# A fp32r decoder trunk: priority for the chain between two projections in the order of VectorE and ScalarE

## The chip, the cores and the metric

The kernel runs on one core of a Trainium2 chip. Its time is the device time of one execution in microseconds. The core has a matmul engine (TensorE, PE in the profile; its weight loads are PEld), a vector engine (VectorE, DVE), a scalar engine (ScalarE, ACT), GpSimd (POOL) and a queue engine (SyncE, SP) that issues DMAs. Each engine works through its own list of instructions in order and waits on semaphores for the others.

## The reference

One inference step of a two-layer trunk of width 1024 over 512 prompt tokens and 8 x 4 sample tokens, in float32. Layer 0 mixes tokens with a gated linear recurrence (RG-LRU, width 1536), layer 1 with a chunked spatial gate. Each is followed by an MLP of width 4096 with a squared ReLU. What matters here stands between two matmuls:

```python
        x = x + g_m * rmsnorm(mix, norm_g[layer, 1])
        hf = rmsnorm(x, norm_g[layer, 2]) * (1.0 + sc_f) + sh_f
        f = jnp.square(jax.nn.relu(hf @ mlp_w_up[layer])) @ mlp_w_down[layer]
        x = x + g_f * rmsnorm(f, norm_g[layer, 3])
```

The output of one projection is normalised over the width, scaled and added to x; x is normalised again, scaled and shifted; only then can the next projection begin. This is called the chain below. It occurs between two projections three times: recurrent block to MLP of layer 0 (site A, about 324 to 357 us), MLP of layer 0 to the spatial gate's input projection (site B, about 752 to 785 us), spatial gate to MLP of layer 1 (site C, about 1010 to 1043 us).

## The kernel before

**Matmuls.** Activations lie with the width on 128 partitions, eight tiles k of 128 x 544 tokens (`X`, `MIX`, `HH`, `HL`). The tokens are two halves of 272 columns, h=0 (prompt) and h=1 (the rest of the prompt, 240 columns, and 32 sample columns). Every product is done in three passes: with `hi` and `lo` the rounded weight and its remainder, and `HH` and `HL` the same of the activation, it adds `hi`·`HH`, `lo`·`HH` and `hi`·`HL` (L119, one 128x128 weight tile by 272 columns). Two outputs of 272 columns share an accumulator tile `acc` of two PSUM banks; there are three such tiles.

**Weights.** SyncE's DMAs bring them in pieces of 512 KB (`raw`). `Unit.pieces` splits each in halves of 512 columns: ScalarE's cast writes `hi` (L181), VectorE's subtraction writes `lo` (L182); 404 of each. `Stream` writes them some 70 matmuls (`LS`) ahead of their use.

**The chain.** `final_proj` adds the last parts of a projection into `MIX` (L746, VectorE), two tiles k at a time; `Stat` squares them (L366, ScalarE), adds the squares up (L378 to L385, VectorE, `sq` and `pt`) and TensorE averages over the partitions (L391, `aux`). `rstd` makes 1/rms in `R` (L413, L414 on ScalarE, L415, L416 on VectorE). `Chain.run` does this for one half h: after `rstd` the residual, per k (L661 and L663 on VectorE; for h=1 the sample columns first, L654 to L656), squares and a second statistic, then per k the `scale` (L449, VectorE), `HH` (L453, ScalarE) and `HL` (L454, VectorE); the sample columns pass through `HSM` (L435 to L445). `first_sweeps` reads `HH` and `HL` k by k, first all of h=0, then all of h=1. The MLP's accumulators are evacuated by ScalarE (`hf`, L1265). At the start of the kernel the same scales and casts make the input of the first projection's x part (`hin_full`), beside `gt`, the evacuation of the gate part (L947), and `MOD`, the shift, which comes from the ada matmuls (L581, L591, L569).

**What sets the order.** The program is written with a clock that counts matmuls; tasks on it write the chain and the splits between the matmuls. The framework's scheduler then simulates the engines and takes, for each engine, among the instructions that are ready the one written first. `high_priority(offset=n)` makes what is written inside count as written n instructions earlier.

Of the kernel before, what the change touches and what calls it, by code (L numbers as in the profile page):

```python
# [80 lines left out]
def trunk_kernel(  # L81
# [266 lines left out]
    class Stat:  # L348
# [7 lines left out]
        def add(self, src, delay=6):  # L356
            i = self.n % 2
            if i == 0:
                self.cur = slot("sq")[:, 0:T].rearrange("p (j n) -> p j n", j=2)
            A.activation(self.cur[:, i], src, AF.Square)  # L360
            self.n += 1
            if i:
                self.q.append((clk.now + delay, self.cur))

        def add2(self, src, q, delay=6):
            A.activation(q, src, AF.Square)  # L366
            self.n += 2
            self.q.append((clk.now + delay, q))

        def pump(self):  # L370
            for i in range(KD // 2):
                while not clk.forced and (len(self.q) <= i or self.q[i][0] > clk.now):
                    yield 2
                q = self.q[i][1]
                if i == 0:
                    acc_ = q
                elif i == 1:
                    V.tensor_tensor(acc_, acc_, q, op=ALU.add)  # L378
                elif i == 2:
# [30 lines left out]
    def rstd(out, ms):  # L410

        t_ = slot("rs")[:, 0:HW]
        A.activation(out, ms, AF.Abs_reciprocal_sqrt, bias=epsc)  # L413
        A.activation(t_, out, AF.Square)  # L414
        V.scalar_tensor_tensor(t_, ms, EPS, t_, op0=ALU.add, op1=ALU.mult)  # L415
        V.scalar_tensor_tensor(out, t_, -3.0, out, op0=ALU.add, op1=ALU.mult)  # L416
# [7 lines left out]
    def smp(ap):  # L424
        return ap.rearrange("p k (s t) -> p k s t", t=TS)

    def smp_mod(m):
        n = m.shape[1]
        return m[:, :, 1:9].rearrange("p k (s o) -> p k s o", o=1).to_broadcast([P, n, NS, TS])
# [26 lines left out]


# [172 lines left out]
    class Chain:  # L630
# [976 lines left out]
```

## Time and profile before

| | us |
|---|---|
| median of 3 runs | 1432.56 (1431.56 to 1432.67) |
| the profiled execution | 1433.34 |
| its span | 1431.6 |
| TensorE busy in the span | 1393.1 (97%) |
| VectorE busy | 702.8 (49%) |
| ScalarE busy | 630.5 (44%) |

The profile is one execution with times from the span's start; the execution takes 1.7 us more than the span. Matmuls are pipelined: one of 272 columns is listed with 0.29 us, and the next one starts 0.125 us after it. The time in square brackets behind a row is what its engine was idle before it, and the arrow names the instruction that ended the wait. The granted clock is TensorE's, 1.00 for 2.4 GHz and 0.50 for 1.2 GHz.

### The profile page before, as it was taken

The numbers are of one execution on the slowest core, as the hardware profiler recorded it, in microseconds if no ns is written. First come the engines' busy times: TensorE is split into PE (matmuls) and PEld (weight loads), VectorE is DVE, ScalarE is ACT, GpSimd is POOL, SyncE is SP. The second block draws the span as 40 slices with busy tenths as digits, with TensorE's granted clock in tenths as the row PEclk, the third lists the DMA queues.
The fourth block names the chain that finished last, engine by engine and source line by source line (L and its number), as shares of the span: only waits on it lengthen the run. The fifth ranks groups of instructions, "written<-read, shape, count | busy, mean of one in ns | idle before, by whom it ended". The sixth has DMA issues, their size and how long they took to land.

```text
span 1431.6 us, 26339 instructions
## 1 busy us (share of the span) xinstructions
PE 1393.1 (97%) x11130; PEld 1298.9 (91%) x11130; DVE 702.8 (49%) x1442; ACT 630.5 (44%) x1154; POOL 41.5 (3%) x76
## 2 busy tenths in 40 slices
PE   8999999997999999999998999999899999999997
PEld 6899989997999999999997867999899999999996
DVE  4767476779422332333349346654972233333334
ACT  4465746846523413414425434432573341432523
POOL 1200000000100000000000200000000000000000
PEclk8999999999999999999999999999999999999998
DMA  9554544221545545543222333122232223222201
GB/s 308 177 175 127 163 151 149 103 89 60 181 154 173 172 155 174 171 155 117 61 87 60 91 96 111 65 71 69 83 101 90 89 89 89 90 89 89 89 1 63
DMA packets 129152, 165.66 MB, mean 116 GB/s; under 512 B 10168, under 2 KB 105416, under 8 KB 129034
## 3 DMA queue, kind: packets, MB, share of 16 engines
q1 hardware_dynamic: 127274, 161.89, 36.0%
q0 software_dynamic: 1760, 2.09, 0.7%
q8 instruction: 87, 1.43, 0.4%
q14 instruction: 31, 0.25, 0.1%
HBM read 161.31 MB, written 2.65 MB: 115 GB/s over the span
## 4 chain that ended last, share of the span: by engine, by line
PE 64%; issue 26%; DVE 6%; ACT 2%; DMA 1%; POOL 0%; SPq 0%; POOLq 0%; ACTq 0%; DVEq 0%
PE acc L119 58%; PE aux L610 3%; DVE lo L182 1%; PE acc L1494 1%; DVE MIX L449 1%; DVE HL L454 1%; DVE X L663 1%; DMA xsr<-in_x_sample_dram 1%; PE aux L1396 0%; PE aux L581 0%; DVE MIX L661 0%; PE aux L391 0%; DVE rs L415 0%; DVE R L416 0%; PE aux L1362 0%
## 5 line engine op out<-in xcount | busy, mean ns | idle before, releaser
L119 PE MATMUL acc<-HH,hi 128*128 128x272 f32 x1776 | 397.5, 292 | 12.3 <-ACT HH L453 11.2
L182 DVE TENSOR_TENSOR lo<-raw,hi 128x512 fp32r<-128x512 f32 (+1 forms) x404 | 263.9, 683 | 269.1 <-ACT hi L181 205.5
L119 PE MATMUL acc<-HH,lo 128*128 128x272 f32 x1776 | 391.7, 291 | 3.4 <-DVE lo L182 3.4
L181 ACT CAST hi<-raw 128x512 fp32r<-128x512 f32 (+1 forms) x404 | 230.2, 613 | 299.8 <-PE acc L119 174.4
L119 PE MATMUL acc<-HL,hi 128*128 128x272 f32 x1776 | 355.4, 289 | 3.3 <-DVE HL L454 3.3
L119 PEld LDWEIGHTS acc<-HH,hi 128*128 128x128 f32 x1776 | 292.2, 190 | 23.7 <-ACT HH L453 14.2
L119 PEld LDWEIGHTS acc<-HH,lo 128*128 128x128 f32 x1776 | 291.2, 190 | 11.6 <-issue 6.7
L119 PEld LDWEIGHTS acc<-HL,hi 128*128 128x128 f32 x1776 | 273.6, 188 | 10.7 <-issue 5.4
L119 PE MATMUL acc<-hh,lo 128*128 128x272 f32 x1024 | 229.8, 290 | 0.0
L119 PE MATMUL acc<-hh,hi 128*128 128x272 f32 x1024 | 229.7, 290 | 0.0
L119 PE MATMUL acc<-hl,hi 128*128 128x272 f32 x1024 | 229.4, 289 | 0.0
L119 PEld LDWEIGHTS acc<-hh,lo 128*128 128x128 f32 x1024 | 168.1, 188 | 3.7 <-issue 3.6
L119 PEld LDWEIGHTS acc<-hh,hi 128*128 128x128 f32 x1024 | 167.9, 188 | 3.9 <-issue 3.8
L119 PEld LDWEIGHTS acc<-hl,hi 128*128 128x128 f32 x1024 | 168.1, 188 | 3.6 <-issue 3.6
L1268 DVE TENSOR_TENSOR hl<-hf,hh 128x544 fp32r<-128x544 f32 (+1 forms) x76 | 47.7, 634 | 175.2 <-ACT hh L1267 175.1
L1265 ACT ACTIVATE hf<-acc 128x544 f32<-128x544 f32 (+1 forms) x76 | 41.2, 551 | 128.0 <-PE acc L119 126.1
L711 DVE TENSOR_TENSOR MIX<-MIX,acc 128x544 f32<-128x544 f32 x44 | 31.5, 717 | 76.0 <-PE acc L119 75.9
L119 PE MATMUL acc<-yh,hi 128*128 128x272 f32 x208 | 52.6, 290 | 0.3 <-ACT MIX L709 0.3
L119 PE MATMUL acc<-yh,lo 128*128 128x272 f32 x208 | 52.5, 291 | 0.0
L119 PE MATMUL acc<-yl,hi 128*128 128x272 f32 x208 | 52.3, 289 | 0.0
L709 ACT COPY MIX<-acc 128x544 f32<-128x544 f32 x32 | 19.6, 612 | 64.1 <-PE acc L119 64.1
L366 ACT ACTIVATE sq<-MIX 128x544 f32<-128x544 f32 x27 | 17.5, 656 | 65.8 <-DVE MIX L746 65.8
(332 smaller groups left out, 1410.8 us busy)
## 6 DMA issues: line engine op xcount, KB each, us to landing
ada<-in_ada_w_dram SPq DMA_DIRECT2D x96, 512.0 KB, 4.8
raw<-in_mlp_w_up_dram SPq DMA_DIRECT2D x64, 512.0 KB, 4.2
raw<-in_mlp_w_down_dram SPq DMA_DIRECT2D x64, 512.0 KB, 4.7
raw<-in_lru_w_in_dram SPq DMA_DIRECT2D x24, 512.0 KB, 4.3
raw<-in_sg_w_in_dram SPq DMA_DIRECT2D x24, 512.0 KB, 4.1
raw<-in_sg_w_out_dram SPq DMA_DIRECT2D x12, 512.0 KB, 4.3
raw<-in_lru_w_out_dram SPq DMA_DIRECT2D x8, 384.0 KB, 3.3
raw<-in_lru_w_out_dram SPq DMA_DIRECT2D x6, 512.0 KB, 5.7
```

The lines of the kernel that those rows point to most:

```text
L119: nc.tensor.matmul(out, lhsT, rhs, start=start, stop=stop)
L181: A.copy(h_, raw[:, c:c + st])
L182: V.tensor_tensor(l_, raw[:, c:c + st], f32(h_), op=ALU.subtract)
L366: A.activation(q, src, AF.Square)
L449: V.scalar_tensor_tensor(wv, X[:, k, c0:c1], Am[:, k, 0:1], R[:, c0:c1], op0=ALU.mult, op1=ALU.mult)
L454: V.scalar_tensor_tensor(HL[:, k, c0:c1], wv, sh[:, k, 0:1], f32(HH[:, k, c0:c1]), op0=ALU.add, op1=ALU.subtract)
L610: nc.tensor.matmul(ps[32 * g:32 * g + 32, :], scT[:, k, :], ts_[g // 2][:, (g % 2) * 512:(g % 2) * 512 + 512], start=(k == 0), stop=(k == ...
L663: V.scalar_tensor_tensor(X[:, j, c0:c1], MIX[:, j, c0:c1], Gm[:, j, 0:1], X[:, j, c0:c1], op0=ALU.mult, op1=ALU.add)
L709: A.copy(mv, ps[:, :, 0:HW])
L711: V.tensor_tensor(mv, mv, ps[:, :, 0:HW], op=ALU.add)
L1265: A.activation(dw, ps, AF.Relu)
L1268: V.tensor_tensor(dl, dw, f32(dh), op=ALU.subtract)
```

## The change

A wrapper gives every instruction that is issued through it a priority offset of 600. `Vp` and `Ap` are VectorE and ScalarE behind this wrapper, and the chain's instructions are issued through them: the squares and adds of `Stat`, `rstd`, the sample columns (`smp_split`, `smp_scale`, `smp_shift`), `scale`, `shift_split`, the residual in `Chain.run`, and the adds and copies from the accumulators in `mix_add` and `final_proj`. The weight splits, the MLP's and the gates' evacuations and all matmuls and DMAs are issued as before.

```diff
+PRIO = 600
+class First:
+    def __init__(self, tc, eng):
+        self.tc, self.eng = tc, eng
+    def __getattr__(self, name):
+        f = getattr(self.eng, name)
+        def call(*args, **kw):
+            with self.tc.high_priority(offset=PRIO):
+                return f(*args, **kw)
+        return call
...
+    Vp, Ap = First(tc, V), First(tc, A)
...
     def shift_split(sh, k, c0, c1):
         wv = MIX[:, k, c0:c1]
-        A.activation(HH[:, k, c0:c1], wv, AF.Identity, bias=sh[:, k, 0:1])
-        V.scalar_tensor_tensor(HL[:, k, c0:c1], wv, sh[:, k, 0:1], f32(HH[:, k, c0:c1]),
+        Ap.activation(HH[:, k, c0:c1], wv, AF.Identity, bias=sh[:, k, 0:1])
+        Vp.scalar_tensor_tensor(HL[:, k, c0:c1], wv, sh[:, k, 0:1], f32(HH[:, k, c0:c1]),
                                op0=ALU.add, op1=ALU.subtract)
...
-                        V.tensor_tensor(mv, mv, ps[i // 2][:, :, 0:HW], op=ALU.add)
+                        Vp.tensor_tensor(mv, mv, ps[i // 2][:, :, 0:HW], op=ALU.add)
```

On each engine the instructions are the same ones; 215 rows of VectorE, 173 of ScalarE and 802 of TensorE stand elsewhere, those of GpSimd and SyncE do not. In the new program a prioritised instruction is listed under the wrapper's line, L60, and other lines are 20 higher (L182 is L202, L119 is L139, L391 is L411).

VectorE at site A, before, around the weight split `lo_473` (the weights of k 4 to 7 for the second pair of output tiles); `sq` and `pt` are the first statistic of h=1, `L415` its rstd three rows after the last one shown:

```order
L382 TENSOR_TENSOR pt_468_3952<-sq_453_3813 128x272
L182 TENSOR_TENSOR lo_470_3964<-raw_449_3769,hi_469_3963 128x512
L454 SCALAR_TENSOR_TENSOR HL_91<-MIX_93,MOD0_95,HH_90 128x272
L746 TENSOR_TENSOR MIX_93<-MIX_93,acc_467_3937 128x2x272
L182 TENSOR_TENSOR lo_473_3995<-raw_450_3771,hi_472_3994 128x512 x2
L384 TENSOR_TENSOR pt_468_3952<-pt_468_3952,sq_471_3992 128x272
L449 SCALAR_TENSOR_TENSOR MIX_93<-X_89,MOD0_95,R_94 128x272
L385 TENSOR_TENSOR pt_468_3952<-pt_468_3952,sq_471_3992 128x272
L449 SCALAR_TENSOR_TENSOR MIX_93<-X_89,MOD0_95,R_94 128x272
L454 SCALAR_TENSOR_TENSOR HL_91<-MIX_93,MOD0_95,HH_90 128x272
L182 TENSOR_TENSOR lo_479_4044<-raw_458_3861,hi_478_4043 128x512
```

The same place now:

```order
L60 SCALAR_TENSOR_TENSOR rs_477_4027<-aux_476_4024,rs_477_4027 128x272
L60 SCALAR_TENSOR_TENSOR HL_91<-MIX_93,MOD0_95,HH_90 128x272
L60 SCALAR_TENSOR_TENSOR R_94<-rs_477_4027,R_94 128x272
L202 TENSOR_TENSOR lo_473_3995<-raw_450_3771,hi_472_3994 128x512
L60 TENSOR_TENSOR us_480_4050<-MIX_93,R_94 128x256
L60 TENSOR_TENSOR MIX_93<-MIX_93,R_94 128x2x240
...
L60 TENSOR_TENSOR MIX_93<-MIX_93 128x2x272
L60 SCALAR_TENSOR_TENSOR X_89<-MIX_93,MOD0_95,X_89 128x240 x2
L60 TENSOR_TENSOR HSM_92<-X_89,MOD0_95 128x256
L60 TENSOR_TENSOR pt_481_4103<-MIX_93 128x272
L202 TENSOR_TENSOR lo_473_3995<-raw_450_3771,hi_472_3994 128x512
L60 TENSOR_TENSOR pt_481_4103<-pt_481_4103,MIX_93 128x272
```

Before, both halves of `lo_473` stand in the middle of h=0's scales. Now the first half stands just before `us` (the start of h=1's residual), and the second behind that residual, the sums of its squares and the first of their folds.

TensorE at site A, before, from the matmul of h=1's first statistic; `acc_474` and `acc_475` are the first two accumulators of the MLP:

```order
L391 MATMUL aux_476_4024<-pt_468_3952,dmean_80 128x272
L119 MATMUL acc_474_4000<-HH_90,hi_464_3925 128x272
L119 MATMUL acc_474_4000<-HH_90,lo_465_3926 128x272
...
L119 MATMUL acc_475_4001<-HH_90,hi_472_3994 128x272
L119 MATMUL acc_475_4001<-HH_90,lo_473_3995 128x272
...
L119 MATMUL acc_474_4000<-HL_91,hi_462_3889 128x272 x4
L119 MATMUL acc_474_4000<-HL_91,hi_464_3925 128x272 x2
L119 MATMUL acc_475_4001<-HL_91,hi_469_3963 128x272 x4
L119 MATMUL acc_475_4001<-HL_91,hi_472_3994 128x272 x2
```

The same place now:

```order
L411 MATMUL aux_476_4024<-pt_468_3952,dmean_80 128x272
...
L139 MATMUL acc_474_4000<-HL_91,hi_462_3889 128x272 x2
L139 MATMUL acc_475_4001<-HH_90,lo_473_3995 128x272
...
L139 MATMUL acc_474_4000<-HL_91,hi_462_3889 128x272 x2
L139 MATMUL acc_474_4000<-HL_91,hi_464_3925 128x272 x4
L139 MATMUL acc_474_4000<-HL_91,hi_462_3889 128x272 x4
L139 MATMUL acc_474_4000<-HL_91,hi_464_3925 128x272 x4
L139 MATMUL acc_498_4203<-HH_90,hi_478_4043 128x272
L139 MATMUL acc_475_4001<-HH_90,lo_473_3995 128x272
```

Before, the matmuls with `lo_473` follow soon after the statistic and all come ahead of the HL matmuls. Now those of its first half come later, then 14 HL matmuls and one with `acc_498` (the third pair of outputs), and then the first one with its second half, the last row.

VectorE at the start of the kernel, before, from the second `R` on:

```order
L416 SCALAR_TENSOR_TENSOR R_94<-rs_74_539,R_94 128x272
L947 TENSOR_TENSOR gt_75_544<-acc_41_277,R_94 128x544
L182 TENSOR_TENSOR lo_77_547<-raw_48_288,hi_76_546 128x512
L867 TENSOR_TENSOR HSM_92<-HSM_92,R_94 128x128
L182 TENSOR_TENSOR lo_79_551<-raw_48_288,hi_78_550 128x512
L449 SCALAR_TENSOR_TENSOR MIX_93<-X_89,MOD0_95,R_94 128x512
L182 TENSOR_TENSOR lo_81_555<-raw_49_290,hi_80_554 128x512
L449 SCALAR_TENSOR_TENSOR MIX_93<-X_89,MOD0_95,R_94 128x512
L182 TENSOR_TENSOR lo_83_559<-raw_49_290,hi_82_558 128x512
L947 TENSOR_TENSOR gt_85_619<-acc_42_278,R_94 128x544
L569 TENSOR_TENSOR MOD0_95<-aux_87_623,G1_164 128x36
L449 SCALAR_TENSOR_TENSOR MIX_93<-X_89,MOD0_95,R_94 128x512
```

The same place now (a sample row and a split left out):

```order
L60 SCALAR_TENSOR_TENSOR R_94<-rs_74_539,R_94 128x272
L60 SCALAR_TENSOR_TENSOR MIX_93<-X_89,MOD0_95,R_94 128x512 x8
L967 TENSOR_TENSOR gt_75_544<-acc_41_277,R_94 128x544
L202 TENSOR_TENSOR lo_77_547<-raw_48_288,hi_76_546 128x512
L887 TENSOR_TENSOR HSM_92<-HSM_92,R_94 128x128
L202 TENSOR_TENSOR lo_79_551<-raw_48_288,hi_78_550 128x512
L202 TENSOR_TENSOR lo_81_555<-raw_49_290,hi_80_554 128x512
L967 TENSOR_TENSOR gt_85_619<-acc_42_278,R_94 128x544
L589 TENSOR_TENSOR MOD0_95<-aux_87_623,G1_164 128x36
L967 TENSOR_TENSOR gt_88_666<-acc_43_279,R_94 128x544
L60 TENSOR_TENSOR HSM_92<-HSM_92,MOD0_95 128x128
L60 SCALAR_TENSOR_TENSOR HL_91<-MIX_93,MOD0_95,HH_90 128x512 x4
```

All eight scales of the x projection's input have moved ahead of `gt`, the splits and the `MOD` that the casts need; before, two stood ahead of `MOD`.

## Rows read from the trace of the kernel before

**Rows 1.** The page, part 1: busy us (share of span), instructions, by engine.
```profile
PE 1393.1 (97%) x11130; PEld 1298.9 (91%) x11130; DVE 702.8 (49%) x1442; ACT 630.5 (44%) x1154; POOL 41.5 (3%) x76
```

**Rows 2.** TensorE's waits: total us, times, longest, by what ended them.
```profile
PE acc L119 <- ACT HH L453: 11.2, 8, 3.0
PE aux L391 <- DVE pt L385: 3.8, 3, 1.8
PE acc L119 <- DVE lo L182: 3.4, 4, 1.0
PE acc L119 <- DVE HL L454: 3.3, 3, 1.1
```

**Rows 3.** Timeline of TensorE, site A: start, duration, [idle before and its releaser].
```profile
323.88 0.29 PE L119 MATMUL acc<-HH,lo 128*128 128x272 f32 x1
...
327.19 0.39 PE L119 MATMUL acc<-HH,hi 128*128 128x272 f32 x1 [3.03 <-ACT HH L453]
...
348.26 0.39 PE L391 MATMUL aux<-pt,dmean 128*128 128x272 f32 x1
...
353.17 0.39 PE L119 MATMUL acc<-HH,hi 128*128 128x272 f32 x1 [0.92 <-ACT HH L453]
...
355.15 0.39 PE L119 MATMUL acc<-HH,hi 128*128 128x272 f32 x1 [0.71 <-ACT HH L453]
```

**Rows 4.** Timeline of VectorE, site A.
```profile
324.11 0.44 DVE L415 SCALAR_TENSOR_TENSOR rs<-aux,rs 128x272 f32<-128x272 f32 x1
324.46 0.72 DVE L378 TENSOR_TENSOR sq<-sq,sq 128x544 f32<-128x544 f32 x1
...
326.08 1.33 DVE L449 SCALAR_TENSOR_TENSOR MIX<-X,MOD,R 128x272 f32<-128x272 f32 x3
...
330.97 1.30 DVE L182 TENSOR_TENSOR lo<-raw,hi 128x512 fp32r<-128x512 f32 x2
...
337.26 0.43 DVE L654 TENSOR_TENSOR us<-MIX,R 128x256 f32<-128x256 f32 x1
...
345.67 0.45 DVE L382 TENSOR_TENSOR pt<-MIX 128x272 f32<-128x272 f32 x1
...
349.90 0.44 DVE L415 SCALAR_TENSOR_TENSOR rs<-aux,rs 128x272 f32<-128x272 f32 x1 [1.54 <-ACT rs L414]
```

**Rows 5.** Timeline of ScalarE, site A: the second evacuation of an MLP accumulator.
```profile
350.98 0.39 ACT L1265 ACTIVATE hf<-acc 128x272 f32<-128x272 f32 x1
```

**Rows 6.** Timelines of VectorE and TensorE, site B.
```profile
766.39 0.41 DVE L654 TENSOR_TENSOR us<-MIX,R 128x256 f32<-128x256 f32 x1
...
781.17 0.62 PE L1396 MATMUL aux<-raw,HSM 128*32 128x512 f32 x1 [0.67 <-DVE HSM L445]
```

**Rows 7.** Timeline of TensorE, site C.
```profile
1013.74 0.39 PE L119 MATMUL acc<-HH,hi 128*128 128x272 f32 x1 [3.02 <-ACT HH L453]
...
1039.73 0.39 PE L119 MATMUL acc<-HH,hi 128*128 128x272 f32 x1 [1.79 <-ACT HH L453]
```

**Rows 8.** Stretches at A and C: us, busy us by engine (x), granted clock, DMA.
```profile
327.19:331.30 4.11, 4.11 (x32) 4.11 (x33) 4.11 (x10) 2.02 (x5) 0.00 (x0) 1.00 0.06 12
1014.86:1018.27 3.41, 3.41 (x18) 3.41 (x17) 3.41 (x8) 1.66 (x4) 0.00 (x0) 0.50 0.11 14
```

**Rows 9.** Timelines of VectorE and TensorE, the start.
```profile
45.32 0.72 DVE L947 TENSOR_TENSOR gt<-acc,R 128x544 f32<-128x544 f32 x1
...
50.53 0.18 DVE L569 TENSOR_TENSOR MOD<-aux,G 128x36 f32<-128x36 f32 x1
...
55.91 2.73 DVE L449 SCALAR_TENSOR_TENSOR MIX<-X,MOD,R 128x512 f32<-128x512 f32 x4
...
53.80 0.42 PE L119 MATMUL acc<-HH,lo 128*128 128x272 f32 x2
...
59.01 1.51 PE L581 MATMUL aux<-ada,scT 128*32 128x128 f32 x46
...
61.41 0.52 PE L119 MATMUL acc<-HH,hi 128*128 128x272 f32 x2 [0.19 <-ACT hi L181]
```

More of the change, by code (lines that the diff above doesn't have):

```diff
@@ L359, in add @@
                 self.cur = slot("sq")[:, 0:T].rearrange("p (j n) -> p j n", j=2)
-            A.activation(self.cur[:, i], src, AF.Square)
+            Ap.activation(self.cur[:, i], src, AF.Square)
             self.n += 1
@@ L365, in add2 @@
         def add2(self, src, q, delay=6):
-            A.activation(q, src, AF.Square)
+            Ap.activation(q, src, AF.Square)
             self.n += 2
@@ L377, in pump @@
                 elif i == 1:
-                    V.tensor_tensor(acc_, acc_, q, op=ALU.add)
+                    Vp.tensor_tensor(acc_, acc_, q, op=ALU.add)
                 elif i == 2:
-                    V.tensor_tensor(acc_, acc_, q, op=ALU.add)
+                    Vp.tensor_tensor(acc_, acc_, q, op=ALU.add)
                     p = slot("pt")
-                    V.tensor_tensor(p[:, 0:HW], acc_[:, 0], acc_[:, 1], op=ALU.add)
+                    Vp.tensor_tensor(p[:, 0:HW], acc_[:, 0], acc_[:, 1], op=ALU.add)
                 else:
-                    V.tensor_tensor(p[:, 0:HW], p[:, 0:HW], q[:, 0], op=ALU.add)
-                    V.tensor_tensor(p[:, 0:HW], p[:, 0:HW], q[:, 1], op=ALU.add)
+                    Vp.tensor_tensor(p[:, 0:HW], p[:, 0:HW], q[:, 0], op=ALU.add)
+                    Vp.tensor_tensor(p[:, 0:HW], p[:, 0:HW], q[:, 1], op=ALU.add)
             if self.rows:
@@ L412, in rstd @@
         t_ = slot("rs")[:, 0:HW]
[L413 to L416, printed above, removed]
+        Ap.activation(out, ms, AF.Abs_reciprocal_sqrt, bias=epsc)
+        Ap.activation(t_, out, AF.Square)
+        Vp.scalar_tensor_tensor(t_, ms, EPS, t_, op0=ALU.add, op1=ALU.mult)
+        Vp.scalar_tensor_tensor(out, t_, -3.0, out, op0=ALU.add, op1=ALU.mult)
     def newton_rstd(out, v, tmp):
@@ L434, in smp_split @@
     def smp_split(k0, k1):
-        A.copy(HH[:, k0:k1, SEQ:T], HSM[:, k0:k1])
-        V.tensor_tensor(HL[:, k0:k1, SEQ:T], HSM[:, k0:k1], f32(HH[:, k0:k1, SEQ:T]), op=ALU.subtract)
+        Ap.copy(HH[:, k0:k1, SEQ:T], HSM[:, k0:k1])
+        Vp.tensor_tensor(HL[:, k0:k1, SEQ:T], HSM[:, k0:k1], f32(HH[:, k0:k1, SEQ:T]), op=ALU.subtract)
     def smp_scale(Am, k0, k1):
@@ L440, in smp_scale @@
         w3 = HSM[:, k0:k1]
-        V.tensor_tensor(smp(w3), smp(X[:, k0:k1, SEQ:T]), smp_mod(Am[:, k0:k1]), op=ALU.mult)
-        V.tensor_tensor(w3, w3, R[:, None, SEQ:T].to_broadcast([P, n, NSMP]), op=ALU.mult)
+        Vp.tensor_tensor(smp(w3), smp(X[:, k0:k1, SEQ:T]), smp_mod(Am[:, k0:k1]), op=ALU.mult)
+        Vp.tensor_tensor(w3, w3, R[:, None, SEQ:T].to_broadcast([P, n, NSMP]), op=ALU.mult)
     def smp_shift(sh, k0, k1):
-        V.tensor_tensor(smp(HSM[:, k0:k1]), smp(HSM[:, k0:k1]), smp_mod(sh[:, k0:k1]), op=ALU.add)
+        Vp.tensor_tensor(smp(HSM[:, k0:k1]), smp(HSM[:, k0:k1]), smp_mod(sh[:, k0:k1]), op=ALU.add)
     def scale(Am, k, c0, c1):
         wv = MIX[:, k, c0:c1]
-        V.scalar_tensor_tensor(wv, X[:, k, c0:c1], Am[:, k, 0:1], R[:, c0:c1], op0=ALU.mult, op1=ALU.mult)
+        Vp.scalar_tensor_tensor(wv, X[:, k, c0:c1], Am[:, k, 0:1], R[:, c0:c1], op0=ALU.mult, op1=ALU.mult)
     def shift_split(sh, k, c0, c1):
         wv = MIX[:, k, c0:c1]
-        A.activation(HH[:, k, c0:c1], wv, AF.Identity, bias=sh[:, k, 0:1])
-        V.scalar_tensor_tensor(HL[:, k, c0:c1], wv, sh[:, k, 0:1], f32(HH[:, k, c0:c1]),
+        Ap.activation(HH[:, k, c0:c1], wv, AF.Identity, bias=sh[:, k, 0:1])
+        Vp.scalar_tensor_tensor(HL[:, k, c0:c1], wv, sh[:, k, 0:1], f32(HH[:, k, c0:c1]),
                                op0=ALU.add, op1=ALU.subtract)
@@ L653, in run @@
                 w3 = w[:, 0:KD * NSMP].rearrange("p (k s) -> p k s", k=KD)
-                V.tensor_tensor(w3, MIX[:, :, SEQ:T], R[:, None, SEQ:T].to_broadcast([P, KD, NSMP]), op=ALU.mult)
-                V.tensor_tensor(smp(w3), smp(w3), smp_mod(Gm), op=ALU.mult)
-                V.tensor_tensor(X[:, :, SEQ:T], X[:, :, SEQ:T], w3, op=ALU.add)
+                Vp.tensor_tensor(w3, MIX[:, :, SEQ:T], R[:, None, SEQ:T].to_broadcast([P, KD, NSMP]), op=ALU.mult)
+                Vp.tensor_tensor(smp(w3), smp(w3), smp_mod(Gm), op=ALU.mult)
+                Vp.tensor_tensor(X[:, :, SEQ:T], X[:, :, SEQ:T], w3, op=ALU.add)
                 yield 8
@@ L713, in final_proj @@
     def final_proj(lhs, rhs, both, groups, l, idx, nxt):
-        A.activation(warm, epsc, AF.Abs_reciprocal_sqrt)
+        Ap.activation(warm, epsc, AF.Abs_reciprocal_sqrt)
         S = [Stat(), Stat(nxt is None)]
@@ L735, in final_proj @@
                         mm3(ps, lhs(m), rhs, (1,), col=0)
-                        V.tensor_tensor(MIX[:, m, HS[1]], MIX[:, m, HS[1]], ps[:, 0, 0:HW], op=ALU.add)
+                        Vp.tensor_tensor(MIX[:, m, HS[1]], MIX[:, m, HS[1]], ps[:, 0, 0:HW], op=ALU.add)
                         S[1].add(MIX[:, m, HS[1]])
```

4 lines of the change are left out of this document (2 added, 2 removed).

## The prediction

> **What bounds the kernel now.** I read the page first. TensorE is busy 97% of the span, VectorE 49%, ScalarE 44% [rows 1]: only TensorE's waits can be won, and whatever makes it wait longer is lost. The view of waits comes next. The waits that end on the chain's instructions are those on ScalarE's HH casts (L453), on the statistic's last add (L385) and on VectorE's HL (L454); a fourth ends on the weight split `lo` (L182) [rows 2]. The timeline of TensorE shows where they stand. At the first seam (recurrent block to MLP, "site A") it waits 3.03 us before the first HH matmul and twice in the h=1 sweep (0.92 and 0.71) [rows 3], and between these once for HL and once for `lo` (1.1 and 1.0 are the longest of [rows 2]). The aux wait of [rows 2] and such waits at site B (MLP to spatial gating) [rows 6] and site C (spatial gating to MLP) [rows 7] bring the groups of [rows 2] to 11.2 + 3.8 + 3.4 + 3.3 = 21.7 us. That is all that the change could win. VectorE's timeline says why they are there: between 324.11 and about 348 it is never idle [rows 4]. On a full engine priority cannot shorten the row of work, only choose who is late.
>
> **What moves.** Every engine issues the same instructions as before, so no duration is added or removed. The front part's rows show what changes place. At site A in the new order VectorE does the whole chain of h=0, then the whole residual of h=1, and the second half of one weight split, `lo_473`, comes only near the end of that residual. TensorE reaches the matmul that reads it much sooner, and it works in order: nothing behind it can run.
>
> **Site A, step by step.** All prices are VectorE's durations in [rows 4] less the 0.09 us by which the next instruction starts early (L415 took 0.44, L378 starts 0.35 later): 0.63 us for a 544-wide add, 0.61 for `lo`, 0.41 for a 272-wide scale or HL, 0.35 for a short add or rstd step.
> (1) The add of the last pair (L746) now stands ahead of L415 of h=0. Its accumulator ends with the matmul at 323.88 + 0.29 = 324.17 [rows 3], so L415 starts at about 324.17 + 0.63 = 324.8, against 324.11: the first HH matmul comes 0.7 us later, 327.9 for 327.19.
> (2) From L415 of h=0 to L654 (the start of h=1's residual) the new order has 2 `lo`, 8 scales, 8 HL and the statistic: 2 x 0.61 + 16 x 0.41 + 2 x 0.63 + 7 x 0.35 = 11.5 us. L654 starts at 336.3 instead of 337.26: a gain of 0.9.
> (3) From L654 to the statistic's folding add (L382) before took 345.67 - 337.26 = 8.4 us, with two HL (0.82) that have now moved ahead and without one 0.34 us sample scale that has moved in: 7.9, and 0.35 for L382 itself. The second `lo_473` starts at about 336.3 + 8.3 = 344.6 and ends at 345.3. Before, that pair of `lo` ran from 330.97 to 332.27 [rows 4].
> (4) TensorE. The first half of `lo_473` stands just ahead of L654, done at 336.4; behind it are 8 matmuls, 14 of HL and one HH, at the pitch of 0.125 us: 336.4 + 23 x 0.125 = 339.3. There it waits until 345.3, **6.0 us idle**, where before no wait on `lo` was longer than 1.0 [rows 2].
> (5) What is left of h=0 then: 8 + 16 + 31 + 16 = 71 matmuls (8.9 us), an aux (0.3) and seven transposes at the same pitch (0.9): 355.4. The h=1 sweep also needs an accumulator, and its evacuation, L1265 at 350.98 before [rows 5], now stands behind all eight HH casts of h=1. The statistic matmul of h=1 comes at 346.7 for 348.26 [rows 3], its rstd at 348.4 for 349.90 [rows 4]; then VectorE needs 0.8 us for R and the sample's product and some 0.37 us (240 wide: between the 0.35 and 0.41 above) for each of 8 scales, 8 HL and four more sample steps, 7.4 us for the 20: 356.6 at the last HL, with the eighth HH just before it on ScalarE and the evacuation right behind. So h=1 starts at about **356.7**, and then without a wait. Before it started at 353.17 and lost 0.87 more inside (0.71 at 355.15 and the slower first matmul after a wait, 0.39 for 0.29) [rows 3], effectively 354.04. Site A: 356.7 - 354.0 = **+2.7 us**. The waits for HL and those of 0.92 and 0.71 us do go; the long one takes their place.
>
> **Sites C and B.** C is A moved by 686.55 us (1013.74 against 327.19). Before, its h=1 sweep started at 1039.73, with the same 0.87 lost inside [rows 7]: 1040.6, against 356.7 + 686.5 = 1043.2 now: **+2.6 us**. At B the second half of `lo_921` has moved behind the residual too. L654 stood at 766.39 there [rows 6]; with the 0.9 us gain, the 8.3 of step 3 and the 0.7 of the `lo` itself it ends near 774.5, and 71 matmuls and an aux (9.2) end h=0 at 783.7, against 781.17 when the sample's matmul started after its wait [rows 6]: **+2.5 us**.
>
> **The start (45 to 64 us).** All eight 512-wide scales (0.66 us pitch, 5.3 us in all [rows 9]) now stand ahead of the gate's evacuation (45.32 before), of four `lo` and of the shift's MOD. Before, MOD came at 50.53 with two scales ahead of it; now at 45.3 + 5.3 + 2 x 0.63 + 4 x 0.61 and two small sample products (0.4 together) = 54.7. MOD releases the HH casts. That is 4.2 later, and the sample's HH and HL, which the second half of the x projection's first matmuls reads, now follow four casts and four HL: 4 x 0.66 plus the HL's own 0.2 and half a microsecond for the casts to get ahead of them, so that the matmul that stood at 53.80 moves to about 54.7 + 0.9 + 3.3 = 58.9, 5.1 later. Given back: the stretch from 59.01 to 61.41 (46 ada matmuls and the waits behind them, 2.4 us), since those matmuls now stand in the wait. Net **+2.7 us** [rows 9]. Bounds: 0 if the casts keep up as before, +5.1 if nothing is given back.
>
> **Elsewhere** (recurrent stretch, last rows) instructions swap places with TensorE dense; nothing late there feeds it, so I take 0, between -1 and +1.
>
> **The clock.** At C the granted clock fell to 0.50 (1.2 GHz) for 3.41 us right after the 3.02 us wait, with 18 matmuls in that stretch where a full stretch of 4.11 us held 32 [rows 8]: 3.41 x 32/4.11 = 26.5, so 8 to 9 matmuls, about 1.1 us, are lost if TensorE is what bounds there. At A a wait of 3.03 us was followed by full clock (1.00) [rows 8]. New waits of 4 us (start) and 6 us (A, B, C) are longer than either. The Trainium skill, "TensorE: Matmul & The Clock Gate", section "Why this matters for your kernels", advises against idle gaps between bursts of matmuls, because the clock then falls back to its lower level. The trace agrees at C and not at A; by the rule all four places would pay, 4.4 us instead of what follows. By the rows: C paid already in before, A hides it (the evacuation, not TensorE, sets the start at 356.7), the start and B pay 1.1 each: **+2 us**, between 0 and 4 x 1.1.
>
> **Sum.** 2.7 + 2.6 + 2.5 + 2.7 + 2 = 12.5 us. On the profiled execution (1433.34, of which 1431.6 is span): 1445.8. The median is 0.8 below that execution: **1445.0 us**, slower by 0.9%.
>
> **Rivals.**
> (a) *The chain wins as meant.* If the late `lo` does not stop TensorE (because the residual runs faster than its durations of before, or the first HH work stretches to cover it), each site keeps the gain of h=1: the statistic of h=1 comes 1.5 us sooner, the HL wait (1.1) and the second wait of the sweep (0.71) go, less the 0.7 of step 1: 2.6 us at three sites, 8 us less with the start at 0: 1425. For it: the waits of [rows 2] are truly those. Against it: VectorE has no idle time in the residual, and step 3 is a sum of measured pitches; the wait would have to shrink by two thirds before the sign turns.
> (b) *Exchange without effect.* The new wait only equals the old ones: the `lo` waits 3 us instead of 6, since 6.0 - 2.7 = 3.3 us is about where site A breaks even; with the start at 0 or 2.7 that gives 1432.6 to 1435.3. For it: the same total of work between the same ends. Against it: the evacuation behind the casts (step 5) holds h=1 back even then.
> (c) *Everything pays.* The long waits are followed by half clock at every place and also shift the following weight splits, which queue behind the second half of the residual: 4.4 us of clock instead of 2, 5.1 at the start instead of 2.7, and one more `lo` wait of 1.0 at each site: 1445 + 2.4 + 2.4 + 3 = 1453.
>
> **How the numbers follow.** Forecast 0.66, (c) 0.16, (a) 0.09, (b) 0.09. The forecast's own range is the bounds of its terms, 1438 to 1451. For 8 in 10 I go a little toward (b): 1436 to 1451. A change of 0.2% (2.9 us) is about what a measurement can tell. Faster by more than that: (a) and a little of (b), 0.11; the same: most of (b), 0.07; slower: 0.82.
>
> **What would show it.** After: one wait of 5 to 6.5 us on `lo` at each of A, B, C, the largest group of the view of waits, where `lo` had 3.4 us in four; HL's 3.3 us gone; the first HH at A 0.5 to 1 us later; h=1 at A starting near 356.7 plus what the start lost; MOD at the start near 54.7. Half clock after the new waits at the start and B. The prediction falls if no wait on `lo` exceeds 3 us, or if TensorE's total idle time grows by less than 5 us.

## The result and the profile after

The changed kernel takes 1443.15 us (median of 4 runs, 1442.40 to 1444.37), the kernel before in the same comparison 1432.06 (1431.10 to 1432.67): a ratio of 1.0084, 95% interval 1.0071 to 1.0097. It is slower by 0.8%. The profiled execution took 1444.37 us, its span 1442.7.

The page's first part answers to [rows 1]: each engine is busy as long as before, TensorE 1.1 us longer. The other 10 of the 11 us between the two spans are TensorE idle.

```profile
PE 1394.2 (97%) x11130; PEld 1303.3 (90%) x11130; DVE 702.7 (49%) x1442; ACT 630.9 (44%) x1154; POOL 41.3 (3%) x76
```

The view of TensorE's waits (total us, times, longest) answers to [rows 2]. HL and the statistic's add have left the list, 7.1 us together, and `lo` leads it with one long wait for each site:

```profile
PE acc L139 <- DVE lo L202: 16.9, 3, 5.7
PE acc L139 <- ACT HH L60: 13.7, 6, 3.7
...
PE acc L139 <- ACT hf L1285: 1.2, 2, 1.1
```

The timeline of TensorE shows them, in order: site A (as [rows 3]), site B, site C (as [rows 7]):

```profile
330.68 0.49 PE L139 MATMUL acc<-HH,hi 128*128 128x272 f32 x1 [3.75 <-ACT HH L60]
...
348.18 0.59 PE L139 MATMUL acc<-HH,lo 128*128 128x272 f32 x1 [5.62 <-DVE lo L202]
...
349.71 1.11 PE L411 MATMUL aux<-pt,dmean 128*128 128x272 f32 x2
...
360.06 0.39 PE L139 MATMUL acc<-HH,hi 128*128 128x272 f32 x1 [0.17 <-ACT hf L1285]
...
780.28 0.59 PE L139 MATMUL acc<-HH,lo 128*128 128x272 f32 x1 [5.71 <-DVE lo L202]
...
1041.39 0.59 PE L139 MATMUL acc<-HH,lo 128*128 128x272 f32 x1 [5.60 <-DVE lo L202]
...
1053.27 0.39 PE L139 MATMUL acc<-HH,hi 128*128 128x272 f32 x1 [1.08 <-ACT hf L1285]
```

VectorE's timeline says what the `lo` of 348.18 waited for. First the start of the kernel (as [rows 9]: eight scales, then `gt` and at last `MOD`), then site A (as [rows 4]): one `lo` at 338.57, the residual, and the second `lo` only at 347.44:

```profile
45.21 5.39 DVE L60 SCALAR_TENSOR_TENSOR MIX<-X,MOD,R 128x512 f32<-128x512 f32 x8
50.52 0.72 DVE L967 TENSOR_TENSOR gt<-acc,R 128x544 f32<-128x544 f32 x1
...
54.60 0.18 DVE L589 TENSOR_TENSOR MOD<-aux,G 128x36 f32<-128x36 f32 x1
...
338.57 0.68 DVE L202 TENSOR_TENSOR lo<-raw,hi 128x512 fp32r<-128x512 f32 x1
339.17 0.42 DVE L60 TENSOR_TENSOR us<-MIX,R 128x256 f32<-128x256 f32 x1
...
347.44 0.68 DVE L202 TENSOR_TENSOR lo<-raw,hi 128x512 fp32r<-128x512 f32 x1
...
351.84 0.44 DVE L60 SCALAR_TENSOR_TENSOR rs<-aux,rs 128x272 f32<-128x272 f32 x1 [0.60 <-ACT rs L60]
```

ScalarE at site A: the eighth HH cast of h=1, and right behind it the evacuation that stood at 350.98 before [rows 5].

```profile
359.23 0.49 ACT L60 ACTIVATE HH<-MIX,MOD 128x240 fp32r<-128x240 f32 x1 [0.26 <-DVE MIX L60]
359.63 0.38 ACT L1285 ACTIVATE hf<-acc 128x272 f32<-128x272 f32 x1
```

The view of stretches (columns as in [rows 8]; the clock is the number in front of the DMA share): half clock sits at the `lo` waits of A and B for 6.8 us each. At C it lasts 3.4 us (1040.80 to 1044.21).

```profile
344.48:351.30 6.82, 3.12 (x12) 2.89 (x13) 6.76 (x14) 2.58 (x5) 0.00 (x0) 0.50 0.25 74
777.97:784.80 6.83, 4.52 (x18) 4.29 (x19) 6.20 (x13) 3.36 (x7) 0.00 (x0) 0.50 0.37 104
```

**Where the 11 us came in.** Every program issues the same 26 statistic matmuls (L391, now L411). I subtracted the start of one in before from the start of the same one in another profile. The 1st (307.31 us before) ends the stretch ahead of site A, the 9th (737.82) what holds A, the 17th (993.85) B, the 25th (1395.52) C. The column `start` is counted from an `ada` matmul at 33.13 to 307.31. Up to 33.13 the orders differ by little more than one HL of the samples, but the profiles differ by up to 2.9 us: half clock lasts 3.4 to 10.2 us there (10.2 before, 6.8 in two pieces after), and even e8_act and e13_residonly, with the order and the half clock of before, reach it 1.0 and 0.9 us earlier. Each profile is one execution. Here for all kernels, in us:

| kernel | start | A | B | C |
|---|---|---|---|---|
| the change | +3.8 | +3.4 | +3.3 | +1.6 |
| e1_resid | +3.3 | +6.5 | +1.1 | +6.2 |
| e2_nostart | +1.0 | +3.4 | +3.8 | +1.6 |
| e3_splits | +10.6 | +7.4 | -0.4 | +5.1 |
| e5_RA | +3.2 | +1.1 | +1.2 | +0.5 |
| e6_pool | +3.3 | +10.1 | +6.2 | +8.7 |
| e7_RNA | +0.9 | +2.0 | +1.3 | -0.4 |
| e8_act | 0.0 | +0.1 | 0.0 | 0.0 |
| e9_h0 | 0.0 | +1.7 | +2.7 | +1.0 |
| e11_fill | +4.0 | +2.6 | +1.8 | +2.0 |
| e12_startonly | +3.3 | +0.1 | 0.0 | 0.0 |
| e13_residonly | 0.0 | +2.0 | +1.9 | +1.0 |

The table counts time, not waits. Over A, B and C together TensorE's waits (from the view of waits) are 22.2 us before and 28.7 in the change, and half clock lasts 6.8 and 23.9 us. In e5_RA (waits 21.8, half clock 17.1), e7_RNA (21.6, 17.1) and e13_residonly (21.6, 20.5) TensorE waits no longer than before: what they still lose there shows as matmuls at half clock.

### The profile page after: what moved, and what is told of

Read it like the earlier page. It is cut to its first block, busy times and chain, and to the rows that moved or that the text cites. A ratio compares the mean times of both kernels' runs of the same rounds, so it can differ in the third digit from the quotient of the medians.

```text
span 1442.7 us, 26337 instructions
## 1 busy us (share of the span) xinstructions
PE 1394.2 (97%) x11130; PEld 1303.3 (90%) x11130; DVE 702.7 (49%) x1442; ACT 630.9 (44%) x1154; POOL 41.3 (3%) x76
## 4 chain that ended last, share of the span: by engine, by line
PE 64%; issue 26%; DVE 7%; ACT 2%; DMA 1%; POOL 0%; SPq 0%; POOLq 0%; DVEq 0%
PE acc L139 57%; PE aux L630 3%; DVE MIX L60 3%; DVE HL L60 1%; DVE X L60 1%; PE acc L1514 1%; DVE lo L202 1%; DMA xsr<-in_x_sample_dram 1%; PE aux L411 0%; PE aux L1416 0%; DVE pt L60 0%; PE aux L601 0%; DVE rs L60 0%; DVE sq L60 0%; DVE R L60 0%
## 5 line engine op out<-in xcount | busy, mean ns | idle before, releaser
L139 PE MATMUL acc<-HH,hi 128*128 128x272 f32 x1776 | 398.4, 293 | 16.4 <-ACT HH L60 13.7
L139 PE MATMUL acc<-HH,lo 128*128 128x272 f32 x1776 | 396.0, 293 | 17.1 <-DVE lo L202 16.9
L202 DVE TENSOR_TENSOR lo<-raw,hi 128x512 fp32r<-128x512 f32 (+1 forms) x404 | 262.5, 682 | 277.1 <-ACT hi L201 212.1
L139 PE MATMUL acc<-HL,hi 128*128 128x272 f32 x1776 | 356.3, 290 | 0.0
L139 PEld LDWEIGHTS acc<-HH,hi 128*128 128x128 f32 x1776 | 294.1, 191 | 26.6 <-ACT HH L60 15.3
L139 PEld LDWEIGHTS acc<-HH,lo 128*128 128x128 f32 x1776 | 293.5, 191 | 25.0 <-DVE lo L202 18.2
L139 PEld LDWEIGHTS acc<-HL,hi 128*128 128x128 f32 x1776 | 275.5, 190 | 7.0 <-issue 5.9
L139 PE MATMUL acc<-hh,hi 128*128 128x272 f32 x1024 | 229.7, 290 | 0.0
L139 PE MATMUL acc<-hh,lo 128*128 128x272 f32 x1024 | 229.6, 290 | 0.0
L139 PE MATMUL acc<-hl,hi 128*128 128x272 f32 x1024 | 229.5, 289 | 0.0
L139 PEld LDWEIGHTS acc<-hh,hi 128*128 128x128 f32 x1024 | 168.0, 188 | 3.9 <-issue 3.8
L139 PEld LDWEIGHTS acc<-hl,hi 128*128 128x128 f32 x1024 | 168.1, 188 | 3.6 <-issue 3.6
L139 PEld LDWEIGHTS acc<-hh,lo 128*128 128x128 f32 x1024 | 168.0, 188 | 3.6 <-issue 3.6
L60 ACT ACTIVATE sq<-MIX 128x544 f32<-128x544 f32 (+1 forms) x37 | 21.4, 593 | 83.4 <-DVE MIX L60 66.6
L139 PE MATMUL acc<-yh,hi 128*128 128x272 f32 x208 | 52.6, 290 | 0.3 <-ACT MIX L729 0.3
L139 PE MATMUL acc<-yh,lo 128*128 128x272 f32 x208 | 52.5, 291 | 0.0
L139 PE MATMUL acc<-yl,hi 128*128 128x272 f32 x208 | 52.3, 289 | 0.0
L729 ACT COPY MIX<-acc 128x544 f32<-128x544 f32 x32 | 19.6, 612 | 64.0 <-PE acc L139 64.0
```

The source lines that it names most:

```text
L60: return f(*args, **kw)
L139: nc.tensor.matmul(out, lhsT, rhs, start=start, stop=stop)
L202: V.tensor_tensor(l_, raw[:, c:c + st], f32(h_), op=ALU.subtract)
L729: A.copy(mv, ps[:, :, 0:HW])
```

## The experiments

Unless a kernel is named otherwise, it is the changed kernel with the edit shown. The kernel before ran beside each on the same chip (medians 1431.87 to 1432.27).

**e1_resid: h=1's residual without priority.**

```diff
+            Vr = V if h == 1 else Vp
-                Vp.tensor_tensor(wv, wv, R[:, None, c0:c1]...
+                Vr.tensor_tensor(wv, wv, R[:, None, c0:c1]...
```

> The changed kernel, but the residual of h=1 (us and the adds into X) is issued without priority; the rest of the chain keeps it. In the order both halves of lo_473 (and of its like at B and C) now stand ahead of us. Theory 1 (the time is lost because a weight split waits behind the residual of h=1): the three waits of 5.6 to 5.7 us on lo go, each site falls back to about what it cost before; what the sites lost was 3.4 + 3.3 + 1.6 = 8.3 us, so about 1443.15 - 7 = 1436 us (1433 to 1438), with 2.7 us of it still lost at the start. Rival (the loss comes from the later first HH, the last pair's add standing ahead of the rstd, and from the accumulators' evacuation behind the casts): no more than 2 us come back, 1441 to 1443.

Measured: 1448.52 us, ratio 1.0115 (1.010 to 1.013), slower than the change, and outside both expectations. The `lo` wait shrank as meant (16.9 to 7.8 us), but the view of waits has a new second row, and TensorE's and ScalarE's timelines show its cause at A: the casts are done at 360.28, the evacuation stands behind them, and TensorE, no longer held up by `lo`, waits for it.

```profile
PE acc L139 <- ACT hf L1286: 11.6, 2, 6.8
PE acc L139 <- DVE lo L202: 7.8, 3, 2.6
```

```profile
359.79 0.49 ACT L60 ACTIVATE HH<-MIX,MOD 128x240 fp32r<-128x240 f32 x1 [0.26 <-DVE MIX L60]
360.19 0.38 ACT L1286 ACTIVATE hf<-acc 128x272 f32<-128x272 f32 x1
```

```profile
360.62 0.59 PE L139 MATMUL acc<-HH,hi 128*128 128x272 f32 x1 [4.84 <-ACT hf L1286]
```

So there are two obstacles one behind the other. That alone would make A no slower than in the change, where TensorE reached the evacuation only 0.17 us early. Two things came on top. Without priority the residual stands behind three splits in a row (337.31 to 339.12 on VectorE), and h=1 starts 1.8 us later than in the change: less what each had lost ahead of A, at 360.62 - 1.49 = 359.13, for 360.06 - 2.73 = 357.33. And the long wait is followed by half clock in h=1's sweep (view of stretches), which the change does not have there:

```profile
360.36:363.78 3.42, 3.16 (x13) 3.06 (x14) 1.39 (x4) 3.23 (x9) 0.00 (x0) 0.50 0.00 0
```

At B, where no such evacuation is waited for, the stage falls from +3.3 to +1.1: there the late `lo`, with the half clock behind it, was the cause.

**e5_RA: in addition, h=1's scale, HH and HL without priority.**

```diff
-        Ap.activation(HH[:, k, c0:c1], wv, ...
+        (A if c0 else Ap).activation(HH[:, k, c0:c1], wv, ...
...
```

> The changed kernel, but of h=1's chain the residual (as in e1_resid) and also scale, HH and HL are issued without priority; h=0 and the statistics keep it. On ScalarE the evacuations of the MLP's accumulators (hf) stand between the HH casts of h=1 again, as before the change. Theory 2 (with the weight split out of the way, what holds h=1 back at A and C is the accumulator, whose evacuation stands behind all eight HH casts: 4.8 and 6.8 us in e1_resid): these two waits go, short waits on HH of 0.7 to 2 us take their place, 1440 us (1437 to 1442), with A and C at 1.5 to 2.5 us each over before. Rival (h=1's casts themselves are late, so that the wait on hf is only renamed a wait on HH): 1446 to 1449.

Measured: 1437.18 us, ratio 1.0035 (1.0023 to 1.0048). The wait for `hf` is gone and all three sites fall to between +0.5 and +1.2. Against e1_resid 11.3 us come back, 11.1 of them at A and C, the two sites with the evacuation behind the casts; against the change, with both obstacles eased, 6.0. What is left in the view of waits is the first HH, 3.7 us as in the change, and a shorter `lo`:

```profile
PE acc L139 <- ACT HH L60: 14.5, 8, 3.7
PE acc L139 <- DVE lo L202: 7.7, 3, 2.7
```

**e7_RNA: e5_RA, and the start (`hin_full`) as before.**

```diff
+        First.on = False   # Vp, Ap plain within hin_full
```

> e5_RA, and hin_full at the start without priority too: the priority is left on h=0's chain, on the statistics and on the adds from the accumulators. Theories 1 and 2: 2 to 3.5 us less than e5_RA, 1437 (1434 to 1439). If priority for h=0's chain were worth anything here, it would come out below 1432.

Measured: 1435.20 us, ratio 1.0024 (1.0014 to 1.0035): 2.0 less than e5_RA, the start's share. What still has priority, h=0's chain, both statistics and the adds from the accumulators, wins nothing: the kernel is 3 us slower than before.

**e2_nostart: the change with only the start as before.**

> The changed kernel, but hin_full (the scales, casts and sample rows at the start) is issued without priority; nothing else. Theory 1: the wait of 3.2 us at 55.6 goes and with it the 2.7 us that the start lost: 1440.4 us (1439.5 to 1441.5), the sites unchanged. Rival (the start's loss is only the other order of the ada matmuls, which is made good later, and the 2.7 us come from the recurrent stretch): 1442.5 to 1443.5.

Measured: 1442.14 us, ratio 1.0067 (1.0052 to 1.0082), between the two expectations, so the total decides nothing. In the stages the start falls from +3.8 to +1.0; of the sites A and C stay and B is 0.5 dearer. The +1.0 that is left is lost ahead of `hin_full`: the `ada` matmuls at 43.59 before start at 41.65 here, 1.9 earlier, and the mark at 33.13 is 2.9 earlier. The change loses the same 1.0 there, e12_startonly does not.

**e12_startonly: before, with priority in `hin_full` alone.**

> The kernel of before with the priority of 600 for hin_full at the start alone (its scales, casts, HL and sample rows). On VectorE all eight scales stand ahead of gt, the four lo and MOD, as in the changed kernel; the sites have their order of before. Theory 1: the start loses by itself what it lost in the changed kernel, 2.5 to 3.8 us: 1435 us (1434.3 to 1436.2). Rival (it is made good behind the start): 1431.5 to 1433.

Measured: 1434.92 us, ratio 1.0028 (1.0016 to 1.0040), as expected; +3.3 at the start and nothing elsewhere. The wait is that of TensorE for the cast that `MOD` releases:

```profile
54.44 0.82 PE L142 MATMUL acc<-HH,hi 128*128 128x272 f32 x2 [3.04 <-ACT HH L63]
```

**e8_act: priority for ScalarE's half alone.**

```diff
-    Vp, Ap = First(tc, V), First(tc, A)
+    Vp, Ap = V, First(tc, A)
```

> The changed kernel with ScalarE's half of the change alone (VectorE's instructions plain, ScalarE's prioritised). VectorE's weight splits stand where they stood before. Theory 1 (VectorE's order is what costs): about 1432 us (1430.5 to 1434). Rival (the casts ahead of the evacuations on ScalarE cost by themselves): 1437 or more.

Measured: 1431.13 us, ratio 0.9998 (0.9988 to 1.0007): no change, so ScalarE's half by itself costs nothing. It is no test of the rival, though. ScalarE's timeline at A has the evacuations between the casts, as before:

```profile
351.61 0.88 ACT L60 ACTIVATE HH<-MIX,MOD 128x240 fp32r<-128x240 f32 x2
352.40 0.38 ACT L1285 ACTIVATE hf<-acc 128x272 f32<-128x272 f32 x1
...
353.60 0.88 ACT L60 ACTIVATE HH<-MIX,MOD 128x240 fp32r<-128x240 f32 x2
```

So ScalarE's half does not by itself put the evacuations behind the casts. VectorE's half alone was not run.

**e9_h0: before, with priority (offset 100) for h=0's second rstd, scale, HH and HL alone.**

> The kernel of before with a priority of 100 for only the second rstd, scale, HH and HL of h=0 at each site. On VectorE all of h=0's chain and then all the weight splits stand ahead of h=1's residual. Theory (VectorE is full between 324 and 348 us, so an order only says who is late): the waits on HL and lo inside h=0 (1.1 and 1.0 us a site) go, the residual of h=1 starts 2 us later but ends as before, TensorE waits longer for HH of h=1: 1432 us (1430 to 1434), no difference that can be measured. Rival (the waits inside h=0 were the loss): 1425 to 1428.

Measured: 1439.92 us, ratio 1.0056 (1.0041 to 1.0071). Both theories were wrong. The `lo` and HL waits shrank to 1.0 and 0.4 us in all, and 3.2 us on the sample's `HSM` at B, longer waits on the statistic and on h=1's casts came in, because the splits now stand ahead of h=1's residual (it starts at 338.51, which is 339.76 in before's time, for 337.26 [rows 4]):

```profile
PE acc L139 <- ACT HH L473: 6.0, 2, 4.3
PE aux L411 <- DVE pt L405: 5.2, 3, 1.9
PE aux L1416 <- DVE HSM L465: 3.2, 1, 3.2
```

Over A to C that is 24.1 us of waits for 22.2 before; the rest of the 5.4 us that the sites lost shows as half clock (23.9 us for 6.8).

**e13_residonly: before, with priority for h=1's residual alone.**

> The kernel of before with the priority of 600 for h=1's residual alone (us, the products and the adds into X). In the order no weight split moves behind it: both halves of lo_473 are already ahead, since h=0's chain has no priority over them. Theory 1: no wait on lo appears, 1432 us (1431 to 1434); it takes both, h=0's chain ahead of the splits and the residual ahead of what is left of them. Rival (the residual's priority by itself makes TensorE wait): 1436 or more.

Measured: 1434.73 us, ratio 1.0022 (1.0012 to 1.0033), a little over the expectation. The waits on `lo` shrank to 0.3 us, as expected, and HL of h=0 is late instead, 7.0 us for 3.3 before [rows 2]. In all TensorE waits no longer than before (sums under the table), so the loss in this profile, the slowest of the eight runs (1437.40 us), shows as half clock. At A it stands behind the wait for HL, where before had full clock:

```profile
PE acc L139 <- DVE HL L474: 7.0, 6, 1.7
```

```profile
344.90:348.31 3.41, 3.41 (x18) 3.41 (x17) 2.65 (x6) 0.00 (x0) 0.00 (x0) 0.50 0.27 82
```

**e3_splits: the change, and the weight splits prioritised too.**

```diff
-                    A.copy(h_, raw[:, c:c + st])
-                    V.tensor_tensor(l_, raw[:, c:c + st], f32(h_), ...
+                    Ap.copy(h_, raw[:, c:c + st])
+                    Vp.tensor_tensor(l_, raw[:, c:c + st], f32(h_), ...
```

> The changed kernel, and the weight splits (hi on ScalarE, lo on VectorE) are given the same priority, so that chain and splits stand to one another as they are written, and both ahead of all else. Theory 1: the waits on lo at the sites and the wait at the start go: about 1432 us (1430 to 1436), the time before the change. Rival (what costs is that the chain and its kind stand ahead of the evacuations, hf and gt, so accumulators come free late): more than 1438.

Measured: 1454.49 us, ratio 1.0159 (1.0142 to 1.0176). The rival is borne out: with casts and splits both first, what has no priority is late, the evacuations. The wait for `MIX` (L729, an evacuation of the recurrent stretch) is part of the +10.6 there.

```profile
PE acc L139 <- ACT hf L1285: 14.9, 2, 7.9
...
PE acc L139 <- ACT MIX L729: 3.1, 2, 2.6
```

**e6_pool: the change, and 18 of the late splits on GpSimd.**

```diff
-                    V.tensor_tensor(l_, ...
+                    (nc.gpsimd if self.pool and self.done >= self.pool - 1 else V).tensor_tensor(l_, ...
```

> The changed kernel with full priority, but of the three units that the first sweep of a site reads, the last three of six lo tiles (lo_473, lo_479, lo_483 and their like, two halves each) are subtracted on GpSimd instead of VectorE. Theory 1: the splits no longer stand behind the chain, VectorE has 6 x 0.61 = 3.7 us less to do per site, the chain's gain shows: the sites now gain 2 to 3 us each against before, the start still loses 2.7: 1423 to 1430 us. Rival (a GpSimd subtraction takes so long, over 2.5 us each, that TensorE waits on it as it did on VectorE; or the two engines slow one another on the same memory): 1436 or more.

Measured: 1460.95 us, ratio 1.0201 (1.0186 to 1.0216), the slowest. GpSimd's timeline at A has five subtractions from 327.53 to 334.92, and VectorE's timeline shows what its own instructions took meanwhile: rstd's last step 1.51 us for 0.44, each of four scales 1.19 for 0.44. The next group, four HL at 335.56 while GpSimd is idle, is back at 0.43 each. So the two engines slow one another, as the rival had it.

```profile
327.53 7.39 POOL L202 TENSOR_TENSOR lo<-raw,hi 128x512 fp32r<-128x512 f32 x5 [99.10 <-ACT hi L201]
```

```profile
327.72 1.51 DVE L60 SCALAR_TENSOR_TENSOR R<-rs,R 128x272 f32<-128x272 f32 x1
329.16 1.78 DVE L60 TENSOR_TENSOR sq<-sq,sq 128x544 f32<-128x544 f32 x1
330.86 4.77 DVE L60 SCALAR_TENSOR_TENSOR MIX<-X,MOD,R 128x272 f32<-128x272 f32 x4
335.56 1.72 DVE L60 SCALAR_TENSOR_TENSOR HL<-MIX,MOD,HH 128x272 fp32r<-128x272 f32 x4
```

**e11_fill: the change, and 16 more matmuls per site inside the `lo` wait.** Their result is not used.

```diff
+                    for j in range(k, k + 2):
+                        for _ in range(2):
+                            nc.tensor.matmul(pf[:, 0:c1 - c0], dmean, X[:, j, c0:c1], start=True, stop=True)
```

> The changed kernel, and 16 more matmuls at each site (the averaging weights times X of h=1, into an aux tile that nobody reads; extra work, no result changed), two behind each add into X of h=1's residual. In the order they stand in front of the matmul that waits for the second half of lo_473, so TensorE has some 5 us of work inside the wait of 5.6 us; 7 HL matmuls move behind the wait. Theory 3 (the half clock after the long wait is part of what A and B lost: 6.8 us at half clock in both): the granted clock stays at 1.00 after the wait, A and B come out about 1 us earlier each, C nearly the same: 1441 us (1440 to 1442.5). Rival (the clock's price is hidden by the wait and by the evacuation, and the extra matmuls only add to it): 1443 to 1446.

Measured: 1441.53 us, ratio 1.0076 (1.0061 to 1.0091), 1.6 below the change. The stretch that had half clock at A keeps 1.00 (view of stretches, first row), as does 775 to 785 at B. At A (TensorE's timeline) the two statistic matmuls take 0.68 us in place of 1.11, and h=1 starts with no wait shown.

```profile
344.48:351.30 6.82, 6.82 (x40) 6.24 (x39) 6.82 (x15) 3.05 (x7) 0.00 (x0) 1.00 0.18 48
775.00:785.00 10.00, 10.00 (x65) 9.52 (x64) 9.87 (x22) 5.56 (x12) 0.00 (x0) 1.00 0.31 85
```

```profile
350.06 0.68 PE L411 MATMUL aux<-pt,dmean 128*128 128x272 f32 x2
...
359.98 0.39 PE L139 MATMUL acc<-HH,hi 128*128 128x272 f32 x1
```

## Why the prediction was right

The forecast was 1445.0 and the time is 1443.15, 0.8% slower as forecast. By its steps, with 2.73 us taken off the times at A for what the stretches ahead had lost:

- **Site A.** Step 1: first HH 330.68 - 2.73 = 327.95 (327.9). Step 3: the second `lo` ends at 348.12 - 2.73 = 345.39 (345.3). Step 4: the idle time is 5.62 (6.0); it began at 339.83 for 339.3. Step 5: eight casts and then the evacuation, h=1 at 357.33 (356.7). The 0.6 us over the forecast goes with the clock, which the forecast had called hidden: half clock lay on the statistic matmuls of h=1 (1.11 us), the rstd behind them came on VectorE at 351.84 - 2.73 = 349.11 (348.4), and the casts and the evacuation came that much later. TensorE was late too: its last work of h=0 ends at 359.89 - 2.73 = 357.16, where step 5 had 355.4, so it waited 0.17 us for the evacuation and not 1.3. Where the clock stays full (e11_fill) h=1 starts at 359.98 - 3.24 = 356.74, and the stage costs +2.6, for +2.7 by the sum.
- **Site B.** 2.5 and 1.1 of clock were forecast, together 3.6; measured +3.3. e11_fill parts it otherwise, about 1.8 for the order and 1.5 for the clock.
- **Site C: the term that was mis-sized.** Forecast +2.6, measured +1.6. h=1 starts 9.41 us into the accumulated loss at 1053.27, that is 1043.86 (1043.2). The error is in before: I subtracted 0.87 us that its sweep lost inside [rows 7], but it lost 2.5 there. Right behind the second wait, the trace of before has half clock (view of stretches, and a later stretch of the same length to compare): 17 matmuls for 30, 13 x 0.125 = 1.6 us. The change does not have this half clock; its sweep runs through. e7_RNA agrees: it costs +2.0 at A, with half clock in h=1's sweep (354.00 to 357.41), and -0.4 at C, where the half clock lies ahead of that sweep (1036.66 to 1040.07). I had read only the half clock of [rows 8] and put the clock at C down as paid.

```profile
1042.16:1045.58 3.42, 3.42 (x17) 3.42 (x16) 3.06 (x9) 2.43 (x7) 0.00 (x0) 0.50 0.02 5
1046.00:1049.42 3.42, 3.42 (x30) 3.42 (x29) 2.54 (x6) 3.34 (x9) 0.00 (x0) 1.00 0.00 0
```

- **The start.** 2.7 and 1.1 of clock were forecast for `hin_full`, together 3.8. `MOD` stands at 54.60 (54.7), but `hin_full` cost 2.8 in the change; the other 1.0 of the +3.8 in the table was lost ahead of it, between 33 and 44 us, where nothing was forecast (e2_nostart keeps it). That the two agree is luck. Alone `hin_full` costs 3.3 in a profile and about 3 in the median (e12_startonly).
- **The clock.** +2 was forecast. It cost something like 0.7 at A and 1.5 at B (the change less e11_fill) and gave 1.6 back at C; what it cost at the start no run separates. The price of 1.1 itself came from a stretch [rows 8] in which half clock cost nothing: the next statistic matmul stands at 1019.98 at C and at 333.44 at A, 686.54 apart, as the first HH are (686.55). At C it only waited less, 0.3 us for 1.8.
- **Rivals.** That VectorE has no slack to give was the argument against (a), and no subset of the change that was tried is faster than before: each moves the wait to another row (`lo`, `hf`, HL, `HSM`). What stood against (b), the evacuation behind the casts, is what e1_resid ran into. Of (c) the half clock came true at all four places, its prices did not: A, B and C lost 8.3 us in all, and no second `lo` wait came in.

It was partly luck that the total came so close: A was 0.7 us too cheap and C 1 us too dear. The sum of the sites with the start and all clock terms, 12.5, stood against 11.0 between the spans, of which 1.07 was gained ahead of 33 us; e8_act, e9_h0 and e13_residonly gain 0.9 to 1.3 there with the order of before. The lower end of the forecast's own range does not follow from its terms: with start and clock at 0 and -1 elsewhere they give 1439.3, not 1438.

Left open: a version that is faster than before, and whether the half clock in e5_RA and e7_RNA causes what they still lose or only goes with it. Not tried were more weight slots, so that the splits could be written before the site begins.

## What to carry to other kernels

Priority cannot make a full engine's work shorter; ask for each instruction that loses its place who waits for it, and for how long its group keeps the engine. Look for a second obstacle behind the first: shortening the late `lo` alone, by taking the priority from the residual, made the kernel slower by 5.4 us, because an evacuation queued behind eight casts held TensorE next, came later still, and the wait for it was followed by half clock. When a stage is compared with before, also count what before itself loses there, its half clock included.

## What the runs showed of the hardware

- GpSimd's subtraction of 128x512 fp32 takes 1.48 us at A in e6_pool (7.39/5, beside VectorE's work) and VectorE's 0.61 in before, and while it runs VectorE's instructions take about one GpSimd instruction each (1.19 to 1.78 us for 0.44 to 0.72). The Trainium skill, "SBUF — State Buffer", section "SBUF: two separate sides", says that a VectorE instruction with two SBUF inputs and a GpSimd instruction that reads SBUF exclude each other for the whole instruction; these rows agree, since the scales, `sq` and `R` all read two tiles.
- The same wait at the same place can be followed by either clock. Before the first HH at A, TensorE waited 3.03 us both in before, where full clock followed [rows 8], and in e13_residonly, where the view of stretches has half clock soon after, at 17 matmuls in 3.41 us. At this place it cost nothing: the statistic matmul that follows (333.44 before, 332.54 + 0.90 here) only waits less (TensorE's timelines of before and of e13_residonly).

```profile
327.83:331.24 3.41, 3.41 (x17) 3.41 (x17) 3.41 (x7) 2.07 (x4) 0.00 (x0) 0.50 0.22 41
```

```profile
333.44 0.72 PE L391 MATMUL aux<-pt,dmean 128*128 128x272 f32 x2 [1.83 <-DVE pt L385]
```

```profile
332.54 0.72 PE L411 MATMUL aux<-pt,dmean 128*128 128x272 f32 x2 [0.30 <-DVE pt L405]
```

- Shorter waits can be followed by half clock too. In e7_RNA two waits at A, 0.92 us before 351.89 and 0.70 before 353.87, were followed by it (view of stretches); in before two of 0.92 and 0.71 at the same place were not [rows 3].

```profile
354.00:357.41 3.41, 3.41 (x16) 3.41 (x17) 3.38 (x9) 2.76 (x8) 0.00 (x0) 0.50 0.00 0
```
